# A batched A·Bᵀ kernel: the store of batch 0 is issued from GpSimd's queue, beside the loads

## The chip, the core and the metric

The kernel runs on one core of a Trainium2 chip. A core has five engines that run their own instruction streams and meet only through semaphores: TensorE (PE, matrix multiply), VectorE (DVE), ScalarE (ACT), GpSimd (POOL) and SyncE (SP). Sixteen DMA engines move data between the chip's memory (HBM) and the on-chip memory (SBUF); they are fed by queues, and an engine that issues transfers has a queue of its own. The metric is the time of one execution on the device in microseconds, as the median of several runs.

## What is computed

Sixteen independent products of 512 x 512 matrices in float32, with the second operand transposed:

```python
def setup_inputs():
    batch, m, k, n = 16, 512, 512, 512
    return {
        "a": np.random.randn(batch, m, k).astype(np.float32),
        "b": np.random.randn(batch, n, k).astype(np.float32),
    }

def reference(a, b):
    return np.matmul(a, b.transpose(0, 2, 1)).astype(np.float32)
```

Read are 2 x 16.8 MB, written 16.8 MB: 50.3 MB in all.

## The kernel before

The batches are worked in eight pairs. A load brings the matrices of one operand for both batches of a pair, 2 MB: load 0 is `a` of pair 0, load 1 is `b` of pair 0, load 2 is `a` of pair 1, and so on to load 15. Loads 0 and 1 are cut in two halves of 1 MB. A store writes one batch, 1 MB: stores 0 to 15. There are seven buffers for loads (`ld`, `NL`) and seven for outputs (`ob`, `NO`), each used in turn.

What an engine does for a pair:

- VectorE casts the loaded float32 to bfloat16 in four pieces for each operand (L155 to L163; `ha` and `wa` hold the two halves of `a`, `hb` and `wb` those of `b`), copies the second halves to where the first ones were (L170, L174), and takes the transposed `b` out of PSUM (`tb`, L175).
- TensorE transposes the pieces by multiplying with an identity (L235) and then multiplies (L254).
- ScalarE takes the transposed `a` out of PSUM (`ta`, L194) and copies the products to the output buffer `ob` (L212). It signals `s_out` twice for a pair: when the first batch is complete, and when the second one is.
- SP issues every transfer, loads and stores alike, in the order that the string `ORDER` gives by hand (L33): an L is the next load, an S the next store. The loop is at L88 to L113. Ahead of a load into a buffer that was used before, SP waits until VectorE has cast what it held (`s_cd`, L96). Ahead of store n it waits for `s_out` to reach n + 1 (L109). SP issues in order, so a wait holds up all that stands behind it in the string, and the transfers of a queue start in the order of issue.
- GpSimd builds the identity, and then only relays. The loop at L118 to L133 goes through the same string: for each load it waits for the landing and passes it to VectorE as `s_go`; for each store whose output buffer is used again (stores 0 to 8) it waits for the landing and passes it to ScalarE as `s_of`. ScalarE starts with seven tokens of `s_of` (L184) and takes two for each pair before it writes `ob` (L203), so that pairs 0 to 2 need none of the relayed ones, and pair 3 needs the first.

The string begins with seven loads, which fill the seven buffers, then has stores 0 and 1, and then loads 7 to 10. SP ends by waiting for the last stores (L114, L268).

Of the kernel before, what the change touches and what calls it, by code (L numbers as in the profile page):

```python
# [10 lines left out]
def kernel(  # L11
# [6 lines left out]
    nc = tc.nc  # L18
    P = 128
    batch, M, K = a.shape  # L20
    _, N, _ = b.shape
    J = M // P
# [6 lines left out]
    NL = 7  # L29
    NO = 7  # L30


    ORDER = "LLLLLLLSSLLLLSLSSLSLSLLSSSSSSSSS"  # L33

    def sbuf(name, shape, dtype):
        return ctx.enter_context(nc.sbuf_tensor(name, shape, dtype))

    def sem(name):
        return tc.alloc_semaphore(name)

    with tc.tile_critical(no_gpsimd_drain=True):  # L41
# [8 lines left out]
        ob = sbuf("ob", [P, NO, J, N], f32)  # L50
# [3 lines left out]
        s_set = sem("s_set")  # L54
        s_ld = [sem(f"s_ld{i}") for i in range(NL)]
        s_second = [sem(f"s_second{i}") for i in range(2)]
        s_st = [sem(f"s_st{i}") for i in range(NO)]

        s_go = sem("s_go")
        s_of = sem("s_of")  # L60
# [12 lines left out]
        s_out = sem("s_out")  # L73
# [5 lines left out]
            out=ident[:], in_=ident[:], compare_op=mybir.AluOpType.not_equal, fill=1.0,  # L79
# [4 lines left out]

        n_ld = n_st = 0
        for what in ORDER:  # L88
            if what == "L":
                u, slot = n_ld // 2, n_ld % NL  # L90
# [21 lines left out]
                ).then_inc(s_st[slot], 16)  # L112
                n_st += 1  # L113
        for n in range(batch - NO, batch - 1):  # L114
            nc.sync.wait_ge(s_st[n % NO], 16 * (n // NO + 1))


        n_ld = n_st = 0  # L118
        for what in ORDER:
            if what == "L":  # L120
                got = nc.gpsimd.wait_ge(s_ld[n_ld % NL], 16 * (n_ld // NL + 1))
                if n_ld < 2:
                    got.then_inc(s_go, 1)
                    nc.gpsimd.wait_ge(s_second[n_ld], 16).then_inc(s_go, 1)
                else:
                    got.then_inc(s_go, 2)
                n_ld += 1
            else:
                if n_st < batch - NO:
                    nc.gpsimd.wait_ge(  # L130
                        s_st[n_st % NO], 16 * (n_st // NO + 1)
                    ).then_inc(s_of, 1)
                n_st += 1  # L133

# [11 lines left out]
        with nc.Fori(0, pairs, engines=[dve]) as u:  # L146
            for x, (h, w, s_c, s_w) in enumerate(
# [4 lines left out]
                if x == 0:  # L152
# [3 lines left out]
                    out=h[:, :J, :], in_=src[:, :J, :HK]  # L156
# [4 lines left out]
                    out=h[:, J:, :], in_=src[:, J:, :HK]  # L161
                ).then_inc(s_c, 1)
                nc.vector.tensor_copy(  # L163
                    out=w[:, J:, :], in_=src[:, J:, HK:]
                ).then_inc(s_w, 1)
            for ko in range(KO):
# [5 lines left out]
                if ko == 1:  # L172
# [3 lines left out]
                    out=tb[:, ko, :],  # L176
# [9 lines left out]
        with nc.Fori(0, pairs, engines=[act]) as u:  # L186
            for ko in range(KO):
# [5 lines left out]
                for e in range(2):  # L193
                    c = nc.scalar.copy(  # L194
                        out=ta[:, ko, e * J * P:(e + 1) * J * P].rearrange(
                            "k (j p h) -> k j p h", j=J, h=2
                        ),
# [6 lines left out]
            for e in range(2):  # L204
                dst = ob[:, bass.ds((u * 2 + e) % NO, 1)].rearrange("m o j n -> m (o j) n")
                for j in range(J):
                    if j < J - 1:
                        nc.scalar.wait_ge(s_mm, j + 1)
                    else:
# [3 lines left out]
                        out=dst[:, j, :].rearrange("m (p j) -> m p j", j=2 * J),  # L213
# [51 lines left out]


    with tc.tile_critical(no_gpsimd_drain=True):
        nc.sync.wait_ge(s_st[(batch - 1) % NO], 16 * ((batch - 1) // NO + 1))  # L268


# [28 lines left out]
```

## Time and profile before

| What | Value |
|---|---|
| Time, median of 4 runs | 127.46 us (126.64 to 127.93) |
| The profiled execution's own time | 127.5 us |
| Its span, first to last instruction | 125.7 us |
| TensorE busy | 92.8 us (74%) |
| VectorE busy | 70.4 us (56%) |
| ScalarE busy | 68.3 us (54%) |
| GpSimd busy | 0.7 us (1%) |
| Mean DMA rate over the span | 400 GB/s |
| Median time from issue to landing, stores | 27.7 us |
| Median time from issue to landing, 2 MB loads | 30.7 us (a), 29.7 us (b) |

An engine's busy time counts its operations, not its waits. The rows of slices give, for 40 equal parts of the span, the busy share of an engine in tenths, and for DMA the mean busy share of the 16 DMA engines and the rate at which they moved data. The time from issue to landing of a transfer includes the time for which it stands in the queue behind older ones. In a row of the timeline stand the start in us, the duration, the engine with its line, the operation with what it writes and reads, and in brackets how long the engine was idle before it.

### The profile page before, as it was taken

The page shows a single profiled execution, that of the slowest core. Times are in us where ns is not written, and L with a number is a line of the kernel's source. Part 1 is how long each engine was busy: PE and PEld are TensorE (multiplying, and loading weights), DVE is VectorE, ACT ScalarE, POOL GpSimd, SP SyncE. Part 2 cuts the span into 40 slices and gives each one's busy share as a digit, 9 for nine tenths or more (in the row PEclk, how much of TensorE's full clock was granted, in tenths as well). Part 3 has the DMA queues.
Part 4 walks back from the last instruction along what each step waited for, and adds up shares of the span by engine and source line. Part 5 has one row for each costly group of instructions (what it writes and reads, how often), then busy time and mean ns, then how long its engine had stood idle before and what let it go on. Part 6 is the DMA issues. An engine that isn't in the chain of part 4 may idle for free. (4 is left out here: it accounts for less than half of the span.)

```text
span 125.7 us, 2407 instructions
## 1 busy us (share of the span) xinstructions
PE 92.8 (74%) x768; PEld 58.2 (46%) x768; DVE 70.4 (56%) x112; ACT 68.3 (54%) x130; POOL 0.7 (1%) x6
## 2 busy tenths in 40 slices
PE   0005299998999899799989998996069998997000
PEld 0005296467447634574475467443068447642000
DVE  0055676937992881988768568352396949600000
ACT  4004132669558945965595679568106459666000
POOL 2000000000000000000000000000000000000000
PEclk9999999999999999999999999999657999999955
DMA  4999999999999999999999999999999999999970
GB/s 96 399 425 438 441 428 428 438 433 422 428 287 396 443 381 454 422 422 422 422 443 428 396 443 412 412 438 425 454 425 428 415 415 425 435 425 420 428 305 23
DMA packets 4896, 50.33 MB, mean 400 GB/s; under 512 B 544, under 2 KB 544, under 8 KB 544
## 3 DMA queue, kind: packets, MB, share of 16 engines
q1 hardware_dynamic: 4896, 50.33, 96.1%
HBM read 33.55 MB, written 16.78 MB: 400 GB/s over the span
## 5 line engine op out<-in xcount | busy, mean ns | idle before, releaser
L254 PE MATMUL ps<-tb,ta 128*128 128x512 bf16 x256 | 58.1, 381 | 0.4
L212 ACT COPY ob<-ps 128x512 f32 x64 | 34.7, 588 | 26.5 <-PE ps L254 26.5
L194 ACT COPY ta<-tp 128x512 bf16<-128x512 bf16 x64 | 32.9, 604 | 20.4 <-PE tp L235 20.4
L254 PEld LDWEIGHTS ps<-tb,ta 128*128 128x128 bf16 x256 | 24.4, 98 | 30.6 <-issue 4.0
L235 PE MATMUL tp<-ident,ha 128*128 128x128 bf16 x256 | 20.2, 236 | 12.8 <-PEq L136 12.8
L235 PE MATMUL tp<-ident,hb 128*128 128x128 bf16 x256 | 19.5, 237 | 9.5 <-PEq L136 9.4
L235 PEld LDWEIGHTS tp<-ident,ha 128*128 128x128 bf16 x256 | 17.5, 107 | 16.0 <-issue 14.3
L175 DVE COPY tb<-tp 128x1024 bf16<-128x1024 bf16 x32 | 21.4, 686 | 5.2 <-DVEq L136 5.1
L235 PEld LDWEIGHTS tp<-ident,hb 128*128 128x128 bf16 x256 | 17.3, 107 | 10.2 <-issue 10.2
L155 DVE CAST hb<-ld 128x1024 bf16 x8 | 5.5, 693 | 13.1 <-DVEq L136 12.9
L155 DVE CAST ha<-ld 128x1024 bf16 x8 | 5.5, 688 | 10.1 <-DVEq L136 10.0
L170 DVE COPY ha<-wa 128x2048 bf16<-128x2048 bf16 x8 | 5.6, 694 | 8.0 <-DVEq L136 7.7
L160 DVE CAST hb<-ld 128x1024 bf16 x8 | 5.5, 689 | 1.1 <-DVEq L136 1.1
L160 DVE CAST ha<-ld 128x1024 bf16 x8 | 5.5, 689 | 1.0 <-DVEq L136 1.0
L174 DVE COPY hb<-wb 128x2048 bf16<-128x2048 bf16 x8 | 5.5, 686 | 0.5 <-DVEq L136 0.5
L163 DVE CAST wa<-ld 128x1024 bf16 x8 | 5.5, 688 | 0.0
L163 DVE CAST wb<-ld 128x1024 bf16 x8 | 5.5, 688 | 0.0
L158 DVE CAST wb<-ld 128x1024 bf16 x8 | 5.5, 687 | 0.0
L158 DVE CAST wa<-ld 128x1024 bf16 x8 | 5.5, 686 | 0.0
L185 ACT ACT_TABLE_LOAD x1 | 1.3, 1283 | 1.1 <-SPq L41 1.1
L78 POOL TENSOR_SCALAR_AFFINE_SELECT ident<-ident 128x128 bf16<-128x128 bf16 x1 | 0.3, 292 | 0.2 <-POOL ident L76 0.2
L76 POOL MEMSET ident<- 128x128 bf16 x1 | 0.2, 204 | 0.5 <-SPq L41 0.5
(5 smaller groups left out, 0.6 us busy)
## 6 DMA issues: line engine op xcount, KB each, us to landing
out_dram<-ob SPq DMA_DIRECT2D x16, 1024.0 KB, 27.7
ld<-in_a_dram SPq DMA_DIRECT2D x7, 2048.0 KB, 30.7
ld<-in_b_dram SPq DMA_DIRECT2D x7, 2048.0 KB, 29.7
ld<-in_a_dram SPq DMA_DIRECT2D x2, 1024.0 KB, 6.3
ld<-in_b_dram SPq DMA_DIRECT2D x2, 1024.0 KB, 10.4
```

The source lines that it names most:

```text
L155: nc.vector.tensor_copy(out=h[:, :J, :], in_=src[:, :J, :HK]).then_inc(s_cd, 1)
L158: nc.vector.tensor_copy(out=w[:, :J, :], in_=src[:, :J, HK:])
L160: nc.vector.tensor_copy(out=h[:, J:, :], in_=src[:, J:, :HK]).then_inc(s_c, 1)
L163: nc.vector.tensor_copy(out=w[:, J:, :], in_=src[:, J:, HK:]).then_inc(s_w, 1)
L170: nc.vector.tensor_copy(out=ha[:], in_=wa[:]).then_inc(s_ca, 1)
L174: nc.vector.tensor_copy(out=hb[:], in_=wb[:]).then_inc(s_cb, 1)
L175: nc.vector.tensor_copy(out=tb[:, ko, :], in_=tp[:, 2 + ko % 2].rearrange("k j p -> k (j p)"),).then_inc(s_eb, 1)
L185: nc.scalar.copy(out=one[:], in_=nc.const_aps.tensor(1.0, (P, 1), f32))
L194: c = nc.scalar.copy(out=ta[:, ko, e * J * P:(e + 1) * J * P].rearrange("k (j p h) -> k j p h", j=J, h=2), in_=tp[:, ko % 2, :, e * HP:(e ...
L212: c = nc.scalar.copy(out=dst[:, j, :].rearrange("m (p j) -> m p j", j=2 * J), in_=ps[:, j, :].rearrange("m (j p) -> m p j", j=2 * J),)
L235: t = nc.tensor.transpose(tp[:, 2 * x + g, j, :], h[:, j, g * P:(g + 1) * P], ident[:])
L254: t = nc.tensor.matmul(ps[:, j, :], ta[:, ko, (e * J + j) * P:(e * J + j + 1) * P], tb[:, ko, :].rearrange("k (j p) -> k j p", j=2 * J)[:, ...
```

## The change

Store 0 leaves SP's order and is issued by GpSimd. In the string one S falls away: seven loads, store 1, and then as before. In both loops the count of stores starts at 1. In GpSimd's loop, after the relay of load 3, there is now a wait for `s_out` to reach 1 and the transfer of `ob[:, 0]` to `out[0]`; after the relay of load 6 there is a wait for the landing of that store (`s_first`), which passes its token to ScalarE. Store 0 no longer counts on output buffer 0's own semaphore, so the values to wait for are worked out by a small function, `landed`, one landing lower for that buffer.

```diff
-    ORDER = "LLLLLLLSSLLLLSLSSLSLSLLSSSSSSSSS"
+    ORDER = "LLLLLLLSLLLLSLSSLSLSLLSSSSSSSSS"
...
+        s_first = sem("s_first")
         s_st = [sem(f"s_st{i}") for i in range(NO)]
+
+        def landed(n):
+            return 16 * (n // NO + (n % NO > 0))
...
-        n_ld = n_st = 0
+        n_ld, n_st = 0, 1
         for what in ORDER:
             if what == "L":
                 u, slot = n_ld // 2, n_ld % NL
...
         for n in range(batch - NO, batch - 1):
-            nc.sync.wait_ge(s_st[n % NO], 16 * (n // NO + 1))
-
-
-        n_ld = n_st = 0
+            nc.sync.wait_ge(s_st[n % NO], landed(n))
+
+
+        n_ld, n_st = 0, 1
         for what in ORDER:
             if what == "L":
                 got = nc.gpsimd.wait_ge(s_ld[n_ld % NL], 16 * (n_ld // NL + 1))
...
                 n_ld += 1
+                if n_ld == 4:
+                    nc.gpsimd.wait_ge(s_out, 1)
+                    nc.gpsimd.dma_start(
+                        out[0].rearrange("(p j) n -> p j n", j=J), ob[:, 0]
+                    ).then_inc(s_first, 16)
+                elif n_ld == NL:
+                    nc.gpsimd.wait_ge(s_first, 16).then_inc(s_of, 1)
             else:
                 if n_st < batch - NO:
                     nc.gpsimd.wait_ge(
-                        s_st[n_st % NO], 16 * (n_st // NO + 1)
+                        s_st[n_st % NO], landed(n_st)
                     ).then_inc(s_of, 1)
                 n_st += 1
...
-        nc.sync.wait_ge(s_st[(batch - 1) % NO], 16 * ((batch - 1) // NO + 1))
+        nc.sync.wait_ge(s_st[(batch - 1) % NO], landed(batch - 1))
```

## The prediction

> **What bounds the kernel now.** I read the slices of the page first, to see which resource is never idle, then the queues, then the load on the DMA engines stretch by stretch, then what the queue issuer (SP) waits for, and last the instructions around the moved store. The slices:
>
> ```profile
> PE   0005299998999899799989998996069998997000
> DMA  4999999999999999999999999999999999999970
> GB/s 96 399 425 438 441 428 428 438 433 422 428 287 396 443 381 454 422 422 422 422 443 428 396 443 412 412 438 425 454 425 428 415 415 425 435 425 420 428 305 23
> ```
>
> A slice is 125.7 / 40 = 3.14 us. The DMA row stands at 9 from the second slice to the 38th, while PE has holes. So the transfers set the time, and the engines follow the loads.
>
> ```profile
> q1 hardware_dynamic: 4896, 50.33, 96.1%
> HBM read 33.55 MB, written 16.78 MB: 400 GB/s over the span
> ```
>
> All 34 transfers stand in one queue, SP's. The change adds no byte to these 50.33 MB and takes none away. The next rows cut the span into stretches; the last two numbers of each are the DMA share and GB/s.
>
> ```profile
> 4.00:34.00 30.00, 20.34 (x170) 14.48 (x171) 19.14 (x30) 12.85 (x25) 0.00 (x0) 1.00 1.01 431
> 34.00:38.00 4.00, 4.00 (x21) 1.76 (x19) 3.71 (x7) 2.72 (x6) 0.00 (x0) 1.00 0.96 297
> 44.00:49.00 5.00, 4.94 (x24) 2.10 (x23) 2.81 (x5) 2.61 (x5) 0.00 (x0) 1.00 1.03 406
> 64.00:80.00 16.00, 14.90 (x145) 9.44 (x143) 12.38 (x20) 11.94 (x24) 0.00 (x0) 1.00 1.01 423
> 80.00:102.00 22.00, 16.33 (x115) 10.11 (x114) 11.38 (x18) 10.51 (x20) 0.00 (x0) 0.84 1.01 429
> 122.00:124.50 2.50, 0.00 (x0) 0.00 (x0) 0.00 (x0) 0.00 (x0) 0.00 (x0) 0.50 0.13 56
> ```
>
> The full rate here is 431 GB/s. At that rate 50.33 MB take 116.8 us; from the first packets at 2.0 us that would end at 118.8, and the last landing is at 124.3 (the last store is issued at 116.3 and needs 8.0 us). The missing 5.5 us are the ramp before 4 us, a dip at 34 to 38 us, worth 4 x (1 - 297/431) = 1.24 us, one at 44 to 49, worth 0.29, smaller ones, and the tail, in which the slower ones of the 16 engines finish alone. Only this, the rate and its dips, can change the time as long as SP's queue never runs empty.
>
> It does not. Store 15 needs 8.0 us from issue to landing where one megabyte takes 1.05 / 431 = 2.4 us, so some 5 us of older work still stand before it; the engine that is ahead of the others reports store 14 done at 118.8, 2.5 us after store 15 is issued.
>
> **The change part by part.** *Store 0 leaves SP's queue.* Before, SP issues it at 26.14, behind loads 4, 5 and 6, and it lands 16.0 us later:
>
> ```profile
> out_dram<-ob SPq DMA_DIRECT2D x1, 1024.0 KB, 16.0
> ```
>
> SP saves one issue (0.34 us, median of the store's line), but its next instruction waits for batch 1, whose store went out 2.2 us later in any case, and loads 7 to 9 follow at 28.7 as now. Nothing on the path: 0.
>
> *GpSimd waits for batch 0 and issues the store.* It does so after relaying load 3 (landed at 23.5), so the wait ends at about 26.1, as SP's did. Queued behind this wait on GpSimd is the relay of load 4, which lands at 28.4. GpSimd has 0.7 us of work in the whole span, none after 1.7 us. The trace has no transfer issued by GpSimd. Its issue cost lies between an SP issue (0.34 us) and whatever holds up the descriptors, and here the Trainium skill has a rule against the change. Rows first, of VectorE:
>
> ```profile
> 25.66 0.69 DVE L163 CAST wb<-ld 128x1024 bf16 x1
> 28.61 0.69 DVE L170 COPY ha<-wa 128x2048 bf16<-128x2048 bf16 x1 [2.26 <-DVEq L136]
> ...
> 32.81 0.68 DVE L155 CAST ha<-ld 128x1024 bf16 x1
> ...
> 35.21 0.69 DVE L155 CAST hb<-ld 128x1024 bf16 x1
> ...
> 44.32 0.68 DVE L155 CAST ha<-ld 128x1024 bf16 x1
> ```
>
> "SBUF — State Buffer", section "Who interferes with whom", says that GpSimd cannot write the descriptors of its transfers while a two-port VectorE copy or cast holds their shared port; the section on bandwidth pools of that page gives 3.1 us in place of 0.62 for such a transfer. These casts would be of that kind. But VectorE is idle for the 2.26 us before 28.61, the very moment of the issue. By the row the issue is clear of it; by the rule at its worst the transfer, and the relay of load 4 behind it, come about 2.5 us later (3.1 - 0.62, an estimate). Load 4 is first used at 32.81, 4.4 us after it lands, so both give 0 on the path. I take the row.
>
> *Store 0 shares the engines with loads 4, 5 and 6.* The trace has only one queue, in which transfers land in order. How two are served I take from the skill, "DMA: Bandwidth & Descriptors", section "Queues, rings and completion order": an engine alternates between its queues packet by packet. By the one-queue rows load 5 lands at 33.3 and load 6 at 39.6; by the rule each waits for at most all of store 0, 2.4 us, so 35.7 and 42.0 (estimates). Load 5 is then relayed at about 36.1 against its use at 35.21: 0.9 us late. Behind it VectorE has 2.4 us of slack before its copy at 40.12, and TensorE's transposes of that operand begin only at 39.75, so this is used up there. Load 6 is used at 44.32 and stays 2 us ahead. From store 1 on, SP's queue holds the same bytes behind the same bytes: load 7 lands at 49.5 as before. End: 0.
>
> *Waits added for the output buffers.* After load 6 GpSimd waits for store 0 to have landed, at 36 to 37 us by the above, so nothing waits. What is queued behind, the token for ScalarE, is one of those that allow the copies of pair 3 at 57.39; with the old order it came at 42.2. If store 0 were late, load 7's relay would stand behind this wait, and it costs only if store 0 lands after 49.5. The renumbered slots and counts move nothing: 0.
>
> *One queue more.* Each of the 16 engines now switches between a load's packets and store 0's. Each engine carries eight 8 KB packets of that store. A switch can cost nothing, or what the present queue shows where loads follow a store: 0.29 us at 44 to 49, 0.30 us for two at 64 to 80 (16 x (1 - 423/431)), 0.10 for two at 80 to 102; mean 0.69 / 5 = 0.14. Eight switches give 0 to 2.3 us, 1.1 by the mean. Below nothing is possible too, since store 0 leaves a pair of stores that is followed by one of these dips. I take 0, because the packet records put the dips elsewhere than in the switches: of 32 load packets that took over 1 us (0.61 is usual), 22 fall between 34.8 and 37.3, in pure loading, 7 behind the pair of stores 0 and 1, 2 behind the pair 3 and 4, and only one behind the three single stores.
>
> The sum is 0 against the profiled execution's own 127.5 us (a span of 125.7 and 1.8 around it), which lies at the median of the runs shown, 127.46.
>
> **The rivals.** *Switching costs (slower).* The store and the loads alternate inside each engine at 27 to 36 us, on the resource that sets the end. At the mean of 0.14 this gives 127.5 + 1.1 = 128.6, at the dearest 129.8; it makes the kernel slower by over 1% from 0.16 us a switch. For it stand the dips above; against it 429 GB/s at 80 to 102, where the engines have drifted apart and loads and stores run side by side.
>
> *The dips go (faster).* The largest dip lies in the seventh load of an unbroken run of loads, the second behind two stores in a row. The change breaks up both. If they are caused by these, 1.24 + 0.29 = 1.5 us come back: 126.0. Against it: nothing in the trace ties the first dip to the queue's contents, and it would be as likely to move as to vanish.
>
> *The store does not go beside the loads.* If an engine serves the new queue only when SP's is empty, GpSimd stands at its wait for store 0, load 7 is not relayed, and the queue runs dry at about 67 us, when the store issued at 37.65 has landed. Pair 3, which started at 49.9, would start some 17 us later: 140 or more. Against it is the skill's rule of alternation.
>
> **How the numbers follow.** The four runs of before lie between 126.64 and 127.93, so I take 1%, 1.3 us, as what can be told from no change. No effect: chance 0.50, with 0.025 beyond the bound on each side. Switching costs: 0.28, with 0.18 over 1%. The dips go: 0.18, with 0.13 over 1%. Starved store: 0.04. So faster 0.155, within 1% 0.60, slower 0.245. The prediction is that of no effect, 127.5. The range reaches up to 129.0, past the mean price of the switches but not to their dearest, and down to 126.2, into the case of the dips; outside lie about 0.08 of the first, 0.08 of the second and the 0.04.
>
> **What would show it.** Right: the second queue shows 1.05 MB, landing about 8 us after an issue near 26 to 27 us; loads 5 and 6 land 2 to 3 us later than now, load 7 at 49.5 as now; the rate at 28 to 36 us stays at 431; SP's wait for batch 1 still ends at 28.3; VectorE's cast at 49.89 does not move. Wrong: a rate under 420 GB/s while both queues are busy (switching), no dip at 34 to 38 (the gain), load 7's cast after 51 us (relay or starvation), or store 15 issued so late that the DMA row falls below 9 ahead of the 38th slice.

## The result: 0.4% faster, and the profile after

| | Before | After |
|---|---|---|
| Median | 127.26 us (61 runs) | 126.83 us (40 runs) |
| Range | 126.64 to 128.12 | 126.13 to 127.51 |
| Ratio, 95% interval | | 0.9963 [0.9951, 0.9976] |
| Span of the profiled execution | 125.7 us | 125.3 us |

The forecast was no effect. The time lies inside the predicted range, but it moved: 0.37% is about 0.47 us, and the interval excludes 1. So what has to be explained is half a microsecond, in a kernel whose DMA engines are never idle.

The rows of slices and the queues of the kernel after:

```profile
DMA  4999999999999999999999999999999999999960
GB/s 89 405 424 429 442 439 429 434 419 361 416 458 405 453 382 429 429 434 439 403 455 403 408 437 411 411 442 411 442 418 445 416 416 429 429 424 426 426 285 18
```

```profile
q1 hardware_dynamic: 4752, 49.29, 94.0%
q0 software_dynamic: 144, 1.05, 2.0%
HBM read 33.55 MB, written 16.78 MB: 402 GB/s over the span
...
out_dram<-ob POOLq DMA_DIRECT2D x1, 1024.0 KB, 12.3
```

The DMA row is as full as before, and the bytes are the same. One megabyte now stands in a second queue, and lands 12.3 us after its issue. The low slice has moved: it was the twelfth (287 GB/s), now it is the tenth, and it is shallower (361). The stretches show it better. In each row, the first numbers are the stretch in us and its length, the last is GB/s. Kernel after:

```profile
26.00:34.00 8.00, 7.45 (x81) 5.09 (x80) 6.01 (x11) 6.17 (x12) 0.13 (x1) 1.00 1.00 398
34.00:38.00 4.00, 4.00 (x24) 1.90 (x22) 2.69 (x5) 2.55 (x5) 0.00 (x0) 1.00 1.02 436
...
44.00:49.00 5.00, 5.00 (x25) 2.25 (x23) 1.74 (x4) 3.24 (x6) 0.00 (x0) 1.00 1.00 406
...
26.00:49.00 23.00, 21.90 (x193) 13.32 (x192) 14.92 (x26) 16.67 (x32) 0.13 (x1) 1.00 1.01 415
```

The dip at 34 to 38 us is gone. In its place 26 to 34 us runs at 398 GB/s, where store 0 now enters. Against 431 GB/s the old dip was worth 1.24 us, the new one is worth 8 x (1 - 398/431) = 0.61. Over the whole stretch from 26 to 49 us the kernel before ran at 402:

```profile
26.00:49.00 23.00, 21.90 (x194) 13.33 (x192) 15.13 (x25) 16.65 (x33) 0.00 (x0) 1.00 1.01 402
```

so it lost 23 x (1 - 402/431) = 1.55 us there, and the changed one 0.85. The gain lies there: 1.5 to 4 us ran at 229 GB/s in both, 4 to 26 at 432 before and 430 after, 49 to 102 at 426 and 425. The compute around the store has not become a limit:

```profile
25.33 0.69 DVE L175 CAST wb<-ld 128x1024 bf16 x1
...
31.70 0.68 DVE L167 CAST ha<-ld 128x1024 bf16 x1
...
35.31 0.69 DVE L167 CAST hb<-ld 128x1024 bf16 x1 [1.12 <-DVEq L148]
...
48.97 0.69 DVE L167 CAST hb<-ld 128x1024 bf16 x1 [3.26 <-DVEq L148]
```

Load 5 lands at 35.0 (33.3 before), and the cast of `hb` waits 1.12 us for it. The last row is the cast that uses load 7: at 48.97, 0.92 us earlier than before (49.89), because loads 7 onwards inherit what the DMA engines saved.

A finer look is possible in the records of single DMA packets. A 16 KB load packet usually takes 0.611 us. I add up what the load packets took beyond that and divide by 16 engines; this is called "the stall" below. Just ahead of the first store it was 1.06 us per engine before. After the change it was 0.53, spread over the last microseconds ahead of store 0 and the first ones beside it; no load packet took over 1 us there, 22 did before.

### The profile page after: what moved, and what is told of

The parts are those of the page before. It is cut to its first block, busy times and chain, and to the rows that moved or that the text cites. A ratio compares the mean times of both kernels' runs of the same rounds, so it can differ in the third digit from the quotient of the medians.

```text
span 125.3 us, 2407 instructions
## 1 busy us (share of the span) xinstructions
PE 92.8 (74%) x768; PEld 58.3 (47%) x768; DVE 70.5 (56%) x112; ACT 68.3 (55%) x130; POOL 1.5 (1%) x7
## 5 line engine op out<-in xcount | busy, mean ns | idle before, releaser
L135 POOL DMA_DIRECT2D out_dram<-ob x1 | 0.8, 818 | 23.6 <-ACT ob L224 23.6
## 6 DMA issues: line engine op xcount, KB each, us to landing
out_dram<-ob POOLq DMA_DIRECT2D x1, 1024.0 KB, 12.3
```

## The experiments

All ratios are to the kernel before, run on the same chip in the same comparison. With 12 runs a ratio's interval is about 0.25% each way, so I repeated the variants that matter. Where repeats are put together below, the interval counts only the scatter within each comparison and is somewhat too narrow, as e5 and the pair of e3 and e13 show. Two theories stood at the start. A: the stall belongs to the first write to HBM of an execution. B: it belongs to engines that turn from a run of loads to a store within one queue. C, that an early store helps as such, came with e3.

**Repeats without an edit (e1, e15: the changed kernel; e5: the kernel before).**

> The changed kernel once more, for a second profile. In the first pair of profiles the load packets lost 1.06 us per engine just ahead of the first store before the change (32 to 40 us) and 0.53 us after it (28 to 36 us). If that is where the gain comes from, the ratio is again 0.995 to 0.998, and again there is no dip near 434 GB/s at 34 to 38 us but one of about 0.5 us at 28 to 31 us. If the dips fall by chance, they lie elsewhere in this profile.

> The kernel before once more. Ratio 1.000 within its interval; it shows how far such a comparison is off when nothing is changed. Its profile is a second sample of the dip at 34 to 38 us (1.06 us per engine in the first one). If the dip belongs to the order of this kernel, it is there again at 0.8 to 1.3 us; if it varies from 0.4 us up, the profiles of single runs cannot carry the explanation.

> The changed kernel, third profile, same chip as e13 and e14: ratio 0.995 to 0.998, stall around the beginning of store 0 at 0.5 to 0.6 us per engine, none ahead of store 1.

Measured: e1 0.9981 [0.9952, 1.0010], e15 0.9956 [0.9931, 0.9982]; stalls around the beginning of store 0 of 0.51 and 0.44 us, and the stretch 26 to 49 at 416 and 417 GB/s. e5 1.0030 [1.0000, 1.0060], with a stall of 0.76 us and 406 GB/s. In e5 the dip is at 34 to 38 again:

```profile
34.00:38.00 4.00, 4.00 (x27) 2.09 (x26) 2.32 (x4) 2.71 (x6) 0.00 (x0) 1.00 0.93 317
```

So the dip belongs to the kernel's order and is not a chance event, but its size varies by almost a third from profile to profile. And e5 shows that a 12-run comparison of two identical kernels can come out 0.3% off. No conclusion below rests on one such ratio.

**Store 0 in one queue, but early (e3, repeated as e13).**

```diff
-    ORDER = "LLLLLLLSSLLLLSLSSLSLSLLSSSSSSSSS"
+    ORDER = "LLLLLSLLSLLLLSLSSLSLSLLSSSSSSSSS"
```

> The kernel before, with store 0 moved ahead of loads 5 and 6 in SP's order: as early as in the changed kernel, but in the one queue. Theory C, what helps is that the first store comes early: 0.3 to 0.6 us below the kernel before. Theory B (turning within one queue) and theory A (first write): the full stall of about 1 us per engine moves to 26 to 30 us, time equal to the kernel before within 0.2 us.

> e3 once more. If the second queue is what pays: ratio 0.999 to 1.001, and stalls of over 1 us per engine in all ahead of and around stores 0 and 1. If being early pays: 0.995 to 0.998, as in e3.

Measured: 0.9968 [0.9944, 0.9992], then 1.0014 [0.9989, 1.0039]; weighted by their intervals 0.9990, plus or minus 0.0017. The two differ by more than their intervals allow, and the gain of the first did not come again. The stretches of e13 (26 to 34 and 38 to 44 us) show two dips in place of one, at store 0 and again at store 1:

```profile
26.00:34.00 8.00, 7.45 (x82) 5.04 (x81) 6.36 (x11) 6.11 (x13) 0.00 (x0) 1.00 1.00 399
38.00:44.00 6.00, 5.10 (x64) 3.67 (x62) 5.49 (x9) 4.39 (x9) 0.00 (x0) 1.00 1.01 396
```

0.59 and 0.49 us. In the packet records of e3 and e13, the stall around store 0, its own packets included, is 0.74 and 0.48 us, and another 0.63 and 0.46 us of stalled loads come ahead of store 1. So early in one queue the dip at store 0 is no larger than behind seven loads; but store 1, 10 us later, gets a second dip, which it has in no profile of the changed kernel. C gets no clear support, though two results so far apart cannot exclude a gain of 0.2%. A in its pure form falls, since a second store is stalled for too.

**Stores 0 and 1 apart in one queue (e7, repeated as e14).**

```diff
-    ORDER = "LLLLLLLSSLLLLSLSSLSLSLLSSSSSSSSS"
+    ORDER = "LLLLLLLSLSLLLSLSSLSLSLLSSSSSSSSS"
```

> The kernel before, one queue, with load 7 between stores 0 and 1. If what helps is only that stores 0 and 1 no longer stand one behind the other (as in the changed kernel, and in e3 and e4, which both came out 0.3% faster): ratio 0.996 to 0.998, with the stall ahead of store 0 still at about 1 us and the one behind the stores (0.38 us in load 7) gone. If what helps is the early or parallel store: ratio 1.000.

> e7 once more (load 7 between stores 0 and 1, one queue). If parting the two stores pays nothing: 0.998 to 1.002; the stall ahead of store 0 at 0.75 to 1.1 us per engine, a third sample of that kind.

Measured: 0.9994 [0.9969, 1.0018] and 0.9971 [0.9948, 0.9994]; together 0.9982, plus or minus 0.0017. The stall ahead of store 0 stays at 0.91 and 0.72 us. The one behind the stores is not gone, as was expected, but split: the load behind store 0 stalls 0.16 and 0.30 us per engine, the one behind store 1 0.19 and 0.10, against 0.38 behind the pair. Parting the two may pay 0.2%; that falls short of the 0.37% of the change, but the intervals overlap.

**The second queue, issued by ScalarE (e6).** ScalarE's loop is peeled for pair 0, and issues the store after the first copy of batch 1.

```diff
+                        if j == 0 and isinstance(u, int):
+                            nc.scalar.wait_ge(s_out, 1)
+                            nc.scalar.dma_start(
+                                out[0].rearrange("(p j) n -> p j n", j=J), ob[:, 0]
+                            ).then_inc(s_first, 16)
...
-                if n_ld == 4:
-                    nc.gpsimd.wait_ge(s_out, 1)
...
+                if n_ld == NL:
                     nc.gpsimd.wait_ge(s_first, 16).then_inc(s_of, 1)
```

> The changed kernel, with store 0 issued from ScalarE's queue in place of GpSimd's, at the same moment (about 26 us). If a second queue beside the loads is what helps, whoever issues it: ratio 0.994 to 0.999 and a stall of about 0.5 us per engine at 26 to 32 us. If it is something of GpSimd's queue: time equal to the kernel before, stall about 1 us.

Measured: 0.9982 [0.9955, 1.0009], stall 0.59 us, 413 GB/s from 26 to 49. ScalarE issued the store at 25.17, and its first packet moved at 29.0:

```profile
25.17 0.39 ACTq L230 DMA_DIRECT2D out_dram<-ob  x1
```

The profile behaves as GpSimd's does; the time fits both a gain as large and none. So the shorter stall is not GpSimd's own; that the time follows was not settled by this run.

**The second queue, late (e4).** In GpSimd's loop the issue of store 0 stands after the relay of load 6.

```diff
-                if n_ld == 4:
+                if n_ld == NL:
                     nc.gpsimd.wait_ge(s_out, 1)
...
-                elif n_ld == NL:
                     nc.gpsimd.wait_ge(s_first, 16).then_inc(s_of, 1)
```

> The changed kernel, with GpSimd issuing store 0 only after load 6 has landed (about 40 us), so that store 1 in SP's queue is the first store of the execution. Theories A and B: the stall of about 1 us per engine is back ahead of store 1 at 34 to 38 us, and the time is that of the kernel before within 0.2 us. If the second queue helped in another way (one store less between the loads of SP's queue), 0.3 to 0.5 us of gain stay.

Measured: 0.9973 [0.9947, 0.9998]. Its stretches from 26 to 49 and from 34 to 38 us:

```profile
26.00:49.00 23.00, 21.90 (x194) 13.31 (x192) 15.00 (x25) 16.67 (x32) 0.67 (x1) 1.00 1.00 405
...
34.00:38.00 4.00, 4.00 (x20) 1.82 (x19) 2.90 (x5) 2.26 (x5) 0.00 (x0) 1.00 0.97 319
```

The dip came back at its old place, ahead of store 1 in SP's queue, as A and B say; the time did not go back. With an interval that nearly reaches 1, this is a warning, not a refutation: either the ratio is as far off as e5's, or a store beside the loads pays in another way too. The trace of e4 shows no gain: on average its 16 engines reported the last store done at 122.5 us, in the kernel before at 122.3.

**A tiny first store (e2, e10), and both together (e16).**

```diff
+        nc.gpsimd.memset(wt[:], 0.0).then_inc(s_one, 1)
...
+        nc.scalar.wait_ge(s_one, 1)
+        nc.scalar.dma_start(
+            out[0].rearrange("(p j) n -> p j n", j=J)[:, 0, :128], wt[:]
+        ).then_inc(s_warm, 16)
```

In e10 and e16 it is `out[batch - 1]`; SP waits for `s_warm` before it stores that batch.

> The kernel before, with a 64 KB store of zeros into batch 0 issued from ScalarE's queue at about 2 us (overwritten later by store 0). Theory A, the stall belongs to the first write to HBM of an execution: the dip at 34 to 38 us is gone and comes at 2 to 5 us instead, where part of it may hide in the ramp; time 0.5 to 1 us below the kernel before, or equal. Theory B, the stall belongs to an engine that turns from a run of loads to stores within one queue: the dip at 34 to 38 us stays at about 1.2 us, time equal or 0.1 us longer.

> As e2, but the 64 KB of zeros go to batch 15's place. In e2 the stall ahead of store 0 was 0.40 us per engine, against 1.06, 0.76, 0.89 and 0.91 where no store had come before it. Theory A (any first write): 0.3 to 0.5 us again. If what counts is that the place of store 0 had been written before: 0.75 us or more. Theory B: 0.75 us or more too.

> The changed kernel with the tiny early store of e10. If the tiny store takes away the part of the stall that belongs to the first write, and the second queue another part: stall of 0.1 to 0.3 us per engine at 26 to 34 us, ratio 0.1 to 0.3% below e15 less the price of the tiny store. If both act on the same part: stall about 0.5 us as in e15, ratio the same or 0.1% above.

Measured: stalls ahead of store 0 of 0.40 us (e2) and 0.45 us (e10) in one queue, where 0.72 to 1.06 was found without a tiny store; 0.28 us in e16. It does not matter which batch's place is written. So part of the stall does belong to the first write (A), and the second queue takes away some of the rest. But the times did not follow: e2 1.0002 [0.9973, 1.0032], e10 127.66 us in one run, e16 0.9991 [0.9963, 1.0018]. The tiny store slows the start: on average over the 16 engines load 4 lands at 28.1 us in all three, at 27.7 to 27.8 in every other profile, so it costs 0.3 us. From 26 to 49 us e2 runs as fast as the changed kernel (418 GB/s):

```profile
26.00:49.00 23.00, 21.90 (x194) 13.29 (x193) 15.25 (x25) 16.65 (x33) 0.00 (x0) 1.00 1.01 418
```

but of the 0.66 us spared ahead of store 0 the start takes 0.3, and a stall of 0.26 us at 91 us, which the kernel before does not have, takes nearly all that is left. In e16 the stall behind store 1 is larger (0.46 us, 387 GB/s from 44 to 49).

**Without stores 0 and 1 (e9).** They are left out; the output lacks two batches.

> Stores 0 and 1 are left out altogether (the output lacks batches 0 and 1); the first store is store 2, behind load 10. One look at the dips. Theory A (the first write of an execution) and theory B (the turn from an unbroken run of loads to a store): no dip at 34 to 38 us, and a stall of 0.8 to 1 us per engine ahead of store 2, which has none in the kernel before. Theory D (the dip belongs to load 6 or to that moment): the dip stays at 34 to 38 us. The time falls by two stores, 4.9 us, if the dip is only moved, by 5.9 if it is gone.

Measured: 121.79 us, one run, 5.9 us below the kernel before beside it (127.65); that is what was expected if the dip is gone, not moved, but one run cannot tell the two apart. No dip at 34 to 38, and one ahead of store 2, whose first packet moves at 56.8. The stretches of e9 from 34 to 38 and from 52 to 58 us:

```profile
34.00:38.00 4.00, 4.00 (x20) 1.86 (x19) 3.39 (x6) 2.52 (x5) 0.00 (x0) 1.00 0.99 422
...
52.00:56.00 4.00, 3.45 (x40) 2.39 (x40) 3.50 (x7) 3.01 (x6) 0.00 (x0) 1.00 1.01 406
56.00:58.00 2.00, 2.00 (x11) 0.94 (x10) 2.00 (x5) 1.10 (x3) 0.00 (x0) 1.00 0.91 360
```

The profile is the clearest of all: the dip goes where the first store goes. It is not load 6's, and not that moment's. It is smaller there (0.37 us of stall in the packets ahead of store 2), which neither theory had said.

**More stores beside the loads (e8, e12: store 1 too; e11, e17: stores 1 and 3 too).** The essential lines of e8, and what e11 adds:

```diff
-    ORDER = "LLLLLLLSLLLLSLSSLSLSLLSSSSSSSSS"
+    ORDER = "LLLLLLLLLLLSLSSLSLSLLSSSSSSSSS"
...
+                elif n_ld == 5:
+                    nc.gpsimd.wait_ge(s_out, 2)
+                    nc.gpsimd.dma_start(
+                        out[1].rearrange("(p j) n -> p j n", j=J), ob[:, 1]
+                    ).then_inc(s_next, 16)
```

```diff
-    ORDER = "LLLLLLLLLLLSLSSLSLSLLSSSSSSSSS"
+    ORDER = "LLLLLLLLLLLSLSLSLSLLSSSSSSSSS"
...
+                elif n_ld == 10:
+                    nc.gpsimd.wait_ge(s_out, 4)
+                    nc.gpsimd.dma_start(
+                        out[3].rearrange("(p j) n -> p j n", j=J), ob[:, 3]
+                    ).then_inc(s_third, 16)
```

> The changed kernel, with store 1 too issued by GpSimd (after the relay of load 4) and taken out of SP's order. If alternation spares the turn from loads to stores and back inside SP's queue, the 0.28 us stall in load 7 behind store 1 goes as well: ratio 0.991 to 0.996. If only the first stall counts: 0.996 as the changed kernel. If alternating costs by the switch: 0.998 or more.

> e8 once more, for a second profile and on the same chip as e11: ratio 0.992 to 0.998; stall ahead of store 0 about 0.6 us per engine, none in load 7.

> As e8 (stores 0 and 1 issued by GpSimd), and store 3 as well, after the relay of load 9, so that no two stores stand one behind the other between SP's loads. If each avoided stall behind a pair of stores gives its size: the 0.34 us stall in load 12 becomes 0 to 0.1, ratio 0.2% below that of e12. If not: the same as e12.

> e11 once more. If each store that is moved beside the loads adds 0.2 to 0.35%, as the changed kernel (0.9963), e8 and e12 (0.9948, 0.9943) and e11 (0.9923) suggest: 0.990 to 0.995. If e11 was a lucky sample and only the first two count: 0.994 to 0.997.

| Stores beside the loads | Ratios | Together |
|---|---|---|
| 0 (e1, e15) | 0.9981, 0.9956 | 0.9967 +- 0.0019 |
| 0, 1 (e8, e12) | 0.9948, 0.9943 | 0.9945 +- 0.0017 |
| 0, 1, 3 (e11, e17) | 0.9923, 0.9945 | 0.9935 +- 0.0020 |

The stall in load 7 behind the stores is gone in e8 and e12 (0.02 us or less, against 0.38 before). Two of e8's stretches:

```profile
34.00:38.00 4.00, 4.00 (x27) 2.07 (x26) 2.27 (x4) 2.71 (x6) 0.00 (x0) 1.00 1.06 453
44.00:49.00 5.00, 5.00 (x25) 2.24 (x24) 2.17 (x4) 3.12 (x7) 0.00 (x0) 1.00 1.00 426
```

At 44 to 49 us the rate is 426, against 406 in the kernel before and in the changed one. But from 26 to 34 us it is lower (386; 398 in the changed kernel), and over the whole stretch e8 and e12 come to 416 and 415, no more than the changed kernel and its repeats (415 to 417):

```profile
26.00:49.00 23.00, 21.90 (x194) 13.26 (x193) 15.67 (x26) 16.65 (x33) 0.53 (x1) 1.00 1.00 416
```

So these profiles do not show where a further gain would lie. The third store brings no gain that can be told from two. It was expected to clear load 12; there the stall stayed at about 0.3 us, and it was load 11 that lost its stall (0.32 us in e12; 0.01 to 0.06 here). All four ratios lie below those of the changed kernel (0.9956 to 0.9981): these versions take about 0.55 to 0.65% less than the kernel before, where the change brought 0.37%. But two stores differ from one by only 0.2%, which is within the noise of the two figures.

Where the tail of e11 ends is worth a look, from 119 to 122 and from 122 to 124.5 us:

```profile
119.00:122.00 3.00, 0.00 (x0) 0.00 (x0) 0.00 (x0) 0.00 (x0) 0.00 (x0) 0.50 0.67 284
122.00:124.50 2.50, 0.00 (x0) 0.00 (x0) 0.00 (x0) 0.00 (x0) 0.00 (x0) 0.50 0.01 3
```

Before, 122 to 124.5 still ran at 56 GB/s. The end is set by the slowest of the 16 engines. Before, the first engine reported the last store done at 121.2 and the last one at 124.3; in the changed kernel 120.7 and 123.9, in e11 120.8 and 122.9. The profile of e11 is that of its fastest run (126.11 us), but e17's, of a usual run, ends alike (10 GB/s from 122 to 124.5). So a mean stall per engine is not yet a time: the slowest engine comes 1.4 to 2.8 us after the mean of the 16, and that distance differs from profile to profile.

The mean is steadier. On average the 16 engines reported the last store done at 122.3 us in both profiles of the kernel before, and at 121.5 to 121.9 in all eight with store 0 early in a second queue and no tiny store. In one queue e3, e13, e7 and e14 lie between (122.3, 121.7, 122.0, 122.0), and the three with a tiny store are at 122.0 to 122.2. So the spared stall does reach the end of the mean engine, 0.4 to 0.8 us earlier; the early store in one queue did so too in one of its two profiles.

## Why the prediction was wrong

*That SP's queue never runs empty, and that only the rate and its dips can change the time*: right. Store 15 was issued at 116.1 and took 7.8 us (8.0 before), so older work still stood before it.

*One queue more*: this is the step that failed. The prediction bounded the switches from below nothing to 2.3 us, took 0, and gave as its reason that the dips lie elsewhere than in the switches; of the rival, it said that nothing in the trace ties the first dip to the queue's contents. e9 ties it: without the first two stores the dip is absent, and one stands ahead of the store that is then the first. The packets of the dip are load packets, so it looked like pure loading; but they are the last ones ahead of a store, and the prediction did not weigh what was coming next in the queue. With the store in a second queue the dip shrinks, in every profile with store 0 there early (0.44 to 0.61 us of stall, against 0.72 to 1.06 where the first store came behind seven loads in SP's queue and no tiny store before it), and there is none ahead of store 1. The term was 0 in the sum; the stretch of 26 to 49 us says -0.7 us, the time -0.47.

*The rivals.* The sign that the prediction named for switching costs, under 420 GB/s while both queues are busy, did come: 413 from the first packet of store 0 at 29.4 us to its landing at 37.6. But the slow part is the beginning, and starts ahead of that packet:

```profile
28.00:29.00 1.00, 0.70 (x12) 0.49 (x9) 1.00 (x3) 1.00 (x3) 0.00 (x0) 1.00 0.93 344
29.00:30.00 1.00, 0.81 (x15) 0.73 (x14) 1.00 (x2) 1.00 (x3) 0.00 (x0) 1.00 0.93 319
```

Store packets start up to 36.3 us, and from 34 to 38 the kernel ran at 436 GB/s with no stall in the load packets. A fixed price for each switch does not fit that. (The prediction also took 431 GB/s as the present rate at 28 to 36 us; the old dip begins inside that stretch, which ran at 420 before and 396 after.) The dips' going was the right direction with too large a size: its sign, no dip at 34 to 38 us, came, but 1.5 us were reckoned for both dips; the first is only halved, and the one behind store 1 remains in part (0.28, 0.12 and 0.23 us of stall in the three profiles, against 0.38 and 0.36 before). The starved store did not occur: store 0 landed within 12.3 us.

*The order of landings*: load 5 at 35.0 (35.7 estimated at most), load 6 at 40.6 (42.0 at most), store 0 later than said: about 8 us after its issue was expected, 12.3 measured. Load 7 landed at 48.6 where 49.5 was expected, 0.9 us earlier; of that 0.4 is left at the last landing (123.9 against 124.3).

*The descriptors and VectorE*: no effect on the path, as said, but the reason was off. In the prediction's own rows the cast of 25.66 runs to 26.35, past the issue expected at 26.1; and after the change GpSimd's issue began at 25.32 with a VectorE cast beside it, not in VectorE's gap:

```profile
25.32 0.82 POOL L135 DMA_DIRECT2D out_dram<-ob  x1 [23.63 <-ACT ob L224]
```

It took 0.82 us and the cast 0.69 as always; in e8 GpSimd issued store 1 at 28.84 in 0.53 us beside VectorE's copies of 0.68 us. The 3.1 us that the Trainium skill ("SBUF — State Buffer", the section on bandwidth pools) gives for a whole transfer held up in this way do not show here. The first packet moved 4.1 us after the issue began, but it took 3.8 us from ScalarE's queue too (e6), so little of that delay is GpSimd's own.

*What stays open.* That stores beside the loads pay is shown by the repeats: without a tiny store, the five ratios of kernels with one queue lie at 0.9968 to 1.0030 (mean 0.9995), and the eight with stores in a second queue, one to three of them, at 0.9923 to 0.9982 (mean 0.9956). That the shorter stall is how they pay is likely from its size and place and from the mean end of the 16 engines, but not shown for the time itself, which the slowest engine sets. Against it stands e4 (old dip and no earlier mean end, yet 0.27% faster). How much of it an early store in one queue would bring is not settled by e3 and e13. Why the first store stalls the loads at all, and why some later turns from loads to a store do so (load 6 to store 1 in e3 and e13) and others do not (load 10 to store 2), no run tells.

## What to carry to other kernels

In a kernel that the DMA engines bound, look at the dips in the rate together with what stands next in the queue, not only with what is moving: here load packets slowed ahead of the first store. When loads and stores share one queue, try the stores that fall into the loads in a second one; here that was worth 0.4% for one store, and 0.55% for two, a step within the noise. Before believing half a percent, run the unchanged kernel against itself, and repeat: single 12-run ratios were off by up to 0.3% here.

## What was not expected of the hardware

- A transfer in a second queue did not start at once while the first queue was full. Store 0 was issued at 25.3 us and its first packet moved at 29.4, after all engines had finished load 4 (28.1) and gone on to load 5. From ScalarE's queue it was nearly the same (issued 25.2, first packet 29.0), so it is not mainly the time that GpSimd needs. Afterwards the two queues alternated: store 0's eight packets per engine took about 7 us among the loads' packets, where eight alone take 2.4.
- The first store of an execution cost a DMA engine 0.4 to 1.1 us of stalled loads on average, wherever it stood (e9). Writing 64 KB at 2 us, at either of the two places tried, about halved it (e2, e10), but cost 0.3 us at the start.
